# A trunk layer's kernel: source order kept in two stretches, and the two parts of x1 laid side by side for the seven products

## Chip, core and metric

The kernel runs on one core of one Trainium2 chip. The metric is device time in microseconds of one execution; the kernel before took a median of 2099.56 us in three runs (2097.77 to 2105.01). The profile shown here is of one further execution.

## What is computed

One decoder layer on 512 positions of width 2048, everything in float32. The part that the change touches is the first normalisation and projection, and the MLP at the end:

```python
def reference(x, attn_norm, w_in, sgu_w, sgu_b, conv_w, q_norm, k_norm, w_out,
              mlp_norm, w_mlp_in, w_mlp_out):
    for l in range(DEPTH):                       # DEPTH = 1
        h = rms_norm(x, attn_norm[l])
        p = h @ w_in[l]                          # 2048 -> 5632
        ...
        x = x + jnp.concatenate([y_a, y_b, y_c], axis=-1) @ w_out[l]
        h = rms_norm(x, mlp_norm[l])
        x = x + jnp.square(jax.nn.relu(h @ w_mlp_in[l])) @ w_mlp_out[l]   # 2048 -> 8192 -> 2048
    return x
```

## The kernel before

All activations lie transposed: 128 of the 2048 features on the partitions, the 512 positions along the free axis. A float32 product is made of three matmuls in the type fp32r: every operand is split into a high part (a cast by ACT, line 242) and a low part (what is left, a subtraction by DVE, line 243), and `mm3` (lines 153 to 157) adds high times high, high times low and low times high into one PSUM bank. So each weight tile needs one ACT instruction and one DVE instruction (`wh` and `wl` in the profile, from the raw tile `wr` or `wq`) before TensorE can use it. x1, the input of the MLP, is kept as `xhl`: first all high parts `xh`, then all low parts `xl`.

`stream` (line 206) runs through a list of groups. Each group is a list of pieces of weights; the loads, casts and subtractions of a piece are written two pieces ahead of its matmuls (`AHEAD`), and three buffers each hold `wr`, `wh` and `wl`. Between the matmuls, `step` takes one small piece of other work from a queue of tasks. The framework's scheduler is free to put the instructions of an engine in another order than that in which they are written; each engine then works its list strictly from the front.

The groups in order, with the stretch of the profile in which TensorE runs them:

- four groups for q and k (the first group loads x itself, splits it, line 245, and the mean squares of x come from a second copy of x, `xn`, that POOL loads, lines 264 to 269), then v, the gating and the convolution, then the output projection: 0 to about 734 us;
- the first product of the MLP, x1 times `w_mlp_in`, 8192 columns. One group of 512 columns, 29 groups of 256 columns in the Strassen-Winograd form (764 to 1345 us) and one last group of 256 columns. A group of this form needs seven products of half-size blocks instead of eight. The sums of x1's blocks are made once (tile `tt`), those of the weights by DVE for each group (lines 798 to 804). `product` (line 811) runs the matmuls: products 0, 1 and 3 have a bank of their own, and one matmul takes the high and the low part of x1 next to each other (512 columns, line 823) and a second adds the low part of the weights (256 columns, line 824). Products 2 and 4 share a bank, and so do 5 and 6; these four use `mm3` with 256 columns. DVE puts the products together in the tile `c` (line 829), of which there is one buffer, and POOL stores it in DRAM as `hd` (line 853);
- the second product, relu squared times `w_mlp_out`, from 1366 us to the end: four chunks of 2048 hidden rows (`c`), four groups of 512 outputs each (`ng`), 16 groups in all. POOL loads a hidden tile from DRAM (`hs<-hd`, or `hr` for the first eight, line 875), DVE squares and scales it (lines 879 and 880), ACT and DVE split it into `hid` or `xhl`. These are the tasks of `hid_tasks` (line 867); those of chunk c+1 are put on the queue at group 1 of chunk c. At the end of a group DVE adds its four banks to `acc` (line 925). There are six banks and a group takes four, so the third of the next group's four column blocks needs one of them back.

Of the kernel before, what the change touches and what calls it, by code (L numbers as in the profile page):

```python
# [15 lines left out]
P = 128  # L16
T = 512
# [23 lines left out]
def trunk_kernel(  # L41
# [46 lines left out]

    def step():
        if tasks:  # L90
            f = tasks.popleft()
            if f is not None:
                f()
# [28 lines left out]
    xh, xl = xhl[:, 0], xhl[:, 1]  # L122
    rstd = cpool.tile([P, TB], F32, name="rstd")
# [5 lines left out]
    def load_w(src, n, first=False):  # L129
# [5 lines left out]
        if first:  # L135
            for k in range(2):
                nc.sync.dma_start(out=first[0][:, k], in_=first[1][:, k])
                nc.sync.dma_start(out=raw[:, k], in_=src[:, k])
            for k in range(2):
                nc.vector.tensor_copy(out=h[:, k], in_=raw[:, k])  # L140
                split_x(k, first[0][:, k], g_attn)
                nc.vector.tensor_tensor(out=l[:, k], in0=raw[:, k], in1=h[:, k].bitcast(F32), op=ALU.subtract)
            return h, l
# [9 lines left out]
    def mm3(ps, a, b, start, stop):  # L153
# [3 lines left out]
        nc.tensor.matmul(ps, lhsT=al, rhs=bh, start=False, stop=stop)  # L157
# [18 lines left out]
    def tr_group(src, nt, mov, close, order=None, before=None, tail=False):  # L176
# [13 lines left out]
        def mm(k, h, l, which=None):  # L190
            for n, (j, ts) in enumerate(parts):
                if which in (None, n):
                    s = slice(j * P, (j + 1) * P)
                    a, b = mov(order[k])
                    mm3(st[n][:, ts], (h[:, s], l[:, s]), (a[:, ts], b[:, ts]), k == 0, k == KT - 1)
# [45 lines left out]
    def split(dst_h, dst_l, src):  # L241
        nc.scalar.copy(out=dst_h, in_=src)  # L242
        nc.vector.tensor_tensor(out=dst_l, in0=src, in1=dst_h.bitcast(F32), op=ALU.subtract)  # L243

    def split_x(k, src, gain):

        nc.scalar.activation(out=xh[:, k], in_=src, func=AF.Copy, scale=gain[:, k:k + 1])
        nc.vector.scalar_tensor_tensor(
            out=xl[:, k], in0=src, scalar=gain[:, k:k + 1], in1=xh[:, k].bitcast(F32), op0=ALU.mult, op1=ALU.subtract,
        )  # L250
# [13 lines left out]
    def x_tokens(i):  # L264
# [3 lines left out]
        nc.gpsimd.dma_start(out=xn_t, in_=xn_v[:, t, half * DH:(half + 1) * DH])  # L268
        return lambda: nc.scalar.activation(out=xn_t, in_=xn_t, func=AF.Square, accum_out=tok[:, t, half:half + 1])
# [104 lines left out]
    def x_chunk(kp):  # L374
# [6 lines left out]
        for n in range(2):  # L381
            split_x(2 * kp + n, xr[:, n], g_attn)

    def x_statistics():
        squares = [x_tokens(i) for i in range(3)]

        def one(i):
            squares[i]()
            if i + 3 < 2 * TB:
                squares.append(x_tokens(i + 3))  # L390

        for i in range(2 * TB):
# [11 lines left out]
    def evac_qk(pss, which, half):  # L404
        gain = q_gain if which == 0 else k_gain
# [322 lines left out]
    def close_out(pss, ng):  # L728

        xg = mlp["xg"]  # L730
        for j in range(4):
# [7 lines left out]
            split_x(n, xg[:, n], g_mlp)  # L739
            tasks.append(lambda n=n: nc.scalar.activation(out=xg[:, n], in_=xg[:, n], func=AF.Copy, scale=g_mlp[:, n:n + 1]))  # L740
        if ng == 3:
            yc["cm"].__exit__(None, None, None)
            mlp["tcm"] = pool("sums")
            tt = mlp["tt"] = mlp["tcm"].__enter__().tile([P, 2, 4, KT // 2, TH], F32R, name="tt")
# [9 lines left out]
    def x_sums(tt, xv, m, j):  # L754
# [5 lines left out]
        split(tt[:, 0, j, s], tt[:, 1, j, s], out)  # L760

    def x_operand(j, m):

        if j < 3:
            k, t = ((0, 0), (1, 0), (1, 1))[j]
            return xhl[:, :, 2 * m + k, t * TH:(t + 1) * TH]
        return mlp["tt"][:, :, j - 3, m]

    class Strassen:
# [41 lines left out]
        def product(self, j, h, l):  # L811
            sp, i = mlp["spool"], self.i
            bank, half = ((0, None), (1, None), (2, 0), (3, None), (2, 1), (4, 0), (4, 1))[j]
            if bank == len(self.banks):
                self.banks.append(main_ps(f"pt{bank}{i}"))
            ps = self.banks[bank]
            pv = ps.rearrange("p (h t) -> p h t", h=2)
# [12 lines left out]

            if j == 0:
# [3 lines left out]
                nc.scalar.copy(out=self.p[0], in_=pv[:, 0])  # L835
                add(self.p[0], pv[:, 1], self.p[0])
                return
            c = self.c
            if j == 1:
                add(c[:, 2], pv[:, 0], self.p[0])  # L840
                add(c[:, 2], pv[:, 1], c[:, 2])
            elif j == 2:
                add(c[:, 0], pv[:, 0], self.p[0])
            elif j == 3:
                nc.scalar.copy(out=self.p[1], in_=pv[:, 0])
                add(self.p[1], pv[:, 1], self.p[1])
# [8 lines left out]
    def close_mlp_in(pss, f0):  # L855

        for j, ps in enumerate(pss):
# [3 lines left out]
            nc.scalar.copy(out=c, in_=ps.rearrange("p (h t) -> p h t", h=2))  # L861
# [5 lines left out]
    def hid_tasks(c, ks, alloc, ahead):  # L867
# [9 lines left out]
        def rest(n):  # L877
            t, k = room.pop(n), ks[n]
            nc.vector.scalar_tensor_tensor(out=t, in0=t, scalar=0.0, in1=t, op0=ALU.max, op1=ALU.mult)
            nc.vector.tensor_tensor(out=t, in0=t, in1=rbc, op=ALU.mult)  # L880
# [7 lines left out]
    def open_last_in():  # L888
        mlp["tcm"].__exit__(None, None, None)
# [124 lines left out]
```

## Time and profile before

| | |
|---|---|
| median of three runs | 2099.56 us |
| profiled execution, own time | 2101.5 us |
| its span | 2099.8 us |
| TensorE (PE) busy | 2067.3 us, 98% |
| VectorE (DVE) busy | 1145.1 us, 55% |
| ScalarE (ACT) busy | 674.7 us, 32% |
| mean granted TensorE clock | 0.992 of full speed |

Busy time of PE counts a matmul from its start to its modelled end, and matmuls overlap; the pace of a stream of matmuls is read from the distance between their starts. PE stands for the matmuls, PEld for the loading of their stationary operands. A number in brackets behind a row of the timeline is the idle time of that engine ahead of it, with the instruction that ended it.

### The profile page before, as it was taken

What the parts mean: (1) busy time and instruction counts of PE and PEld (TensorE: products, weight loads), DVE (VectorE), ACT (ScalarE), POOL (GpSimd) and SP (SyncE); (2) the same over time, 40 slices, a digit from 0 to 9 for tenths busy, and PEclk for the clock granted to TensorE, in tenths of its full rate; (3) what the DMA queues carried; (4) which work ended last, traced back from release to release, by engine and by line L of the source; (5) the groups of instructions that cost most, each with busy time, mean ns of one, the idle gap of its engine ahead of it and who ended that gap; (6) DMA issues with size and microseconds to landing.
All of it is one profiled execution on the core that took longest, in us unless ns stands there. A gap on an engine that the chain in (4) does not pass through costs nothing.

```text
span 2099.8 us, 27447 instructions
## 1 busy us (share of the span) xinstructions
PE 2067.3 (98%) x11202; PEld 1807.8 (86%) x11202; DVE 1145.1 (55%) x1530; ACT 674.7 (32%) x905; POOL 100.6 (5%) x194
## 2 busy tenths in 40 slices
PE   9999999999999999999999999999989998999999
PEld 8999888888888889999999999977878887888888
DVE  5443453534335578878888788767372254322222
ACT  6233442322234434334333343432221222221221
POOL 1000000100000000000000000131010010000000
PEclk9999999999999999999999999999999999999999
DMA  8223222433533454444444444474343343233332
GB/s 276 90 76 111 71 71 68 128 96 96 188 119 126 125 161 131 131 140 122 140 131 124 138 131 126 127 254 151 112 150 96 95 133 112 92 101 97 114 120 81
DMA packets 247023, 259.81 MB, mean 124 GB/s; under 512 B 11748, under 2 KB 179940, under 8 KB 246896
## 3 DMA queue, kind: packets, MB, share of 16 engines
q1 hardware_dynamic: 229888, 206.08, 32.6%
q0 software_dynamic: 14560, 47.75, 6.5%
q10 hardware_dynamic: 2448, 4.23, 0.6%
q8 instruction: 88, 1.44, 0.3%
q14 instruction: 39, 0.32, 0.0%
HBM read 232.81 MB, written 25.19 MB: 123 GB/s over the span
## 4 chain that ended last, share of the span: by engine, by line
PE 79%; issue 16%; DMA 3%; POOL 1%; DVE 1%; SPq 0%; ACT 0%; POOLq 0%; DVEq 0%; ACTq 0%
PE pt L155 17%; PE pt L156 17%; PE pt L157 17%; PE pt L823 8%; PE pn L155 5%; PE pn L157 5%; PE pn L156 5%; PE pt L824 4%; DMA hs<-hd 1%; POOL hs L875 1%; DMA hd<-cn 1%; PE sc L505 0%; DMA wr<-in_w_in_dram 0%; PE et L518 0%; DVE wl L243 0%
## 5 line engine op out<-in xcount | busy, mean ns | idle before, releaser
L243 DVE TENSOR_TENSOR wl<-wr,wh 128x1024 fp32r<-128x1024 f32 (+2 forms) x287 | 321.4, 1120 | 652.8 <-ACT wh L242 596.5
L242 ACT CAST wh<-wr 128x1024 fp32r<-128x1024 f32 (+2 forms) x287 | 277.8, 968 | 799.6 <-PE pt L156 661.9
L155 PE MATMUL pt<-xhl,wh 128*128 128x512 f32 (+1 forms) x1144 | 419.6, 367 | 6.0 <-DVE acc L925 6.0
L156 PE MATMUL pt<-xhl,wh 128*128 128x512 f32 (+1 forms) x1144 | 418.3, 366 | 0.0
L157 PE MATMUL pt<-xhl,wl 128*128 128x512 f32 (+1 forms) x1144 | 418.1, 365 | 0.0
L155 PEld LDWEIGHTS pt<-xhl,wh 128*128 128x128 f32 x1144 | 216.5, 189 | 41.3 <-DVE acc L925 6.4
L157 PEld LDWEIGHTS pt<-xhl,wl 128*128 128x128 f32 x1144 | 216.4, 189 | 34.7
L156 PEld LDWEIGHTS pt<-xhl,wh 128*128 128x128 f32 x1144 | 216.6, 189 | 34.4 <-issue 0.2
L242 ACT CAST wh<-wq 128x1024 fp32r<-128x1024 f32 x145 | 152.0, 1048 | 250.7 <-PE pt L156 146.1
L243 DVE TENSOR_TENSOR wl<-wq,wh 128x1024 fp32r<-128x1024 f32 x145 | 177.0, 1221 | 91.2 <-ACT wh L242 91.1
L155 PE MATMUL pt<-hid,wh 128*128 128x512 f32 x512 | 201.7, 394 | 14.7 <-DVE acc L925 14.7
L157 PE MATMUL pt<-hid,wl 128*128 128x512 f32 x512 | 201.3, 393 | 2.1 <-DVE wl L243 2.0
L156 PE MATMUL pt<-hid,wh 128*128 128x512 f32 x512 | 201.2, 393 | 0.0
L155 PE MATMUL pt<-tt,wh 128*128 128x256 f32 x696 | 197.0, 283 | 0.3 <-DVE c L829 0.3
L157 PE MATMUL pt<-tt,wl 128*128 128x256 f32 x696 | 197.1, 283 | 0.0
L156 PE MATMUL pt<-tt,wh 128*128 128x256 f32 x696 | 197.0, 283 | 0.0
L155 PE MATMUL pn<-wh,xhl 128*128 128x384 f32 (+2 forms) x512 | 187.3, 368 | 4.4 <-DVE wh L140 3.8
L156 PE MATMUL pn<-wl,xhl 128*128 128x384 f32 (+2 forms) x512 | 180.4, 352 | 0.0
L157 PE MATMUL pn<-wh,xhl 128*128 128x384 f32 (+2 forms) x512 | 180.2, 352 | 0.0
L823 PE MATMUL pt<-xhl,wh 128*128 128x512 f32 x464 | 165.2, 398 | 0.0
L155 PEld LDWEIGHTS pt<-tt,wh 128*128 128x128 f32 x696 | 132.7, 191 | 3.1 <-issue 0.6
L157 PEld LDWEIGHTS pt<-tt,wl 128*128 128x128 f32 x696 | 132.9, 191 | 0.0
(210 smaller groups left out, 2933.5 us busy)
## 6 DMA issues: line engine op xcount, KB each, us to landing
wr<-in_w_mlp_out_dram SPq DMA_DIRECT2D x128, 512.0 KB, 3.6
wq<-in_w_mlp_in_dram SPq DMA_DIRECT2D x116, 512.0 KB, 4.1
wr<-in_w_in_dram SPq DMA_DIRECT2D x144, 128.0 KB, 2.4
wr<-in_w_out_dram SPq DMA_DIRECT2D x32, 512.0 KB, 3.6
hd<-c POOLq DMA_DIRECT2D x58, 256.0 KB, 2.6
hs<-hd POOLq DMA_DIRECT2D x56, 256.0 KB, 3.4
wr<-in_w_in_dram SPq DMA_DIRECT2D x24, 512.0 KB, 3.5
wr<-in_w_in_dram SPq DMA_DIRECT2D x31, 384.0 KB, 3.2
```

The costliest lines, as they stand in the source:

```text
L155: nc.tensor.matmul(ps, lhsT=ah, rhs=bh, start=start, stop=False)
L156: nc.tensor.matmul(ps, lhsT=ah, rhs=bl, start=False, stop=False)
L157: nc.tensor.matmul(ps, lhsT=al, rhs=bh, start=False, stop=stop)
L242: nc.scalar.copy(out=dst_h, in_=src)
L243: nc.vector.tensor_tensor(out=dst_l, in0=src, in1=dst_h.bitcast(F32), op=ALU.subtract)
L823: nc.tensor.matmul(pv, lhsT=h[:, m], rhs=b, start=start, stop=False)
L824: nc.tensor.matmul(pv[:, 1], lhsT=l[:, m], rhs=b[:, 0], start=False, stop=stop)
L875: nc.gpsimd.dma_start(out=room[n], in_=hd[c * KC + ks[n]])
```

## The change

Three things are changed. `ordr` marks instructions so that the scheduler keeps them in the order of the source: in the first group (until its results are evacuated) and from the opening of the last group of the first product to the end. The loads of `xn` are written singly, each tied behind the last matmul written before it (`behind`), and the squares that use them come two steps later. In the MLP the memory of `xhl` is seen as `x1v`, in which for each feature block and each half of the positions the 256 high values are followed at once by the 256 low values; `tt` gets the same form. All seven products of a group now use one matmul of 512 columns and one of 256, each in a bank of its own, and DVE adds both halves of each bank (`take`). The two plain groups of the first product read x1 through `x1mov`, as two runs of 256.

```diff
@@ load_w, split, split_x
-                nc.vector.tensor_copy(out=h[:, k], in_=raw[:, k])
-                split_x(k, first[0][:, k], g_attn)
+                ordr(nc.vector.tensor_copy(out=h[:, k], in_=raw[:, k]))
+                split_x(xh[:, k], xl[:, k], first[0][:, k], g_attn[:, k:k + 1])
...
+    def ordr(ins):
+        return tc.keep_in_program_order(ins) if ordered[0] else ins
...
+    x1v = xhl.rearrange("p s k t -> p (s k t)").rearrange("p (k h s t) -> p k h s t", k=KT, h=2, s=2)
@@ x_tokens, x_statistics
-        nc.gpsimd.dma_start(out=xn_t, in_=xn_v[:, t, half * DH:(half + 1) * DH])
+        behind(nc.gpsimd.dma_start(out=xn_t, in_=xn_v[:, t, half * DH:(half + 1) * DH]))
...
+            if i < 2 * TB:
+                squares.append(x_tokens(i))
+            if i >= 2:
+                squares[i - 2]()
@@ x_operand
-            return xhl[:, :, 2 * m + k, t * TH:(t + 1) * TH]
-        return mlp["tt"][:, :, j - 3, m]
+            return x1v[:, 2 * m + k, t]
+        return mlp["tt"][:, j - 3, m]
+
+    def x1mov(k):
+        return x1v[:, k, :, 0], x1v[:, k, :, 1]
@@ Strassen.product
-            bank, half = ((0, None), (1, None), (2, 0), (3, None), (2, 1), (4, 0), (4, 1))[j]
...
+            pv = main_ps(f"pt{j}{i}").rearrange("p (h t) -> p h t", h=2)
             for m in range(KT // 2):
+
                 b = x_operand(self.FACTOR[j], m)
-                start, stop = m == 0, m == KT // 2 - 1
-                if half is None:
-
-                    nc.tensor.matmul(pv, lhsT=h[:, m], rhs=b, start=start, stop=False)
-                    nc.tensor.matmul(pv[:, 1], lhsT=l[:, m], rhs=b[:, 0], start=False, stop=stop)
-                else:
-                    mm3(pv[:, half], (h[:, m], l[:, m]), (b[:, 0], b[:, 1]), start, stop)
+                nc.tensor.matmul(pv, lhsT=h[:, m], rhs=b, start=m == 0, stop=False)
+                nc.tensor.matmul(pv[:, 1], lhsT=l[:, m], rhs=b[:, 0], start=False, stop=m == KT // 2 - 1)
...
+            def take(out, more):
+                add(out, pv[:, 0], more)
+                add(out, pv[:, 1], out)
...
             elif j == 2:
-                add(c[:, 0], pv[:, 0], self.p[0])
+                take(c[:, 0], self.p[0])
...
             elif j == 4:
-                add(c[:, 1], pv[:, 1], c[:, 0])
+                take(c[:, 1], c[:, 0])
                 add(c[:, 0:6:5], self.p[1].unsqueeze(1).broadcast_to([P, 2, TH]), c[:, 0:2])
+            elif j == 5:
+                take(c[:, 3], c[:, 0])
             elif j == 6:
-                add(c[:, 3:5], pv, c[:, 0:2])
+                take(c[:, 4], c[:, 1])
@@ groups
-    groups.append(tr_group(w1[:, :, :T], 4, xmov, lambda pss: close_mlp_in(pss, 0)))
+    groups.append(tr_group(w1[:, :, :T], 4, x1mov, lambda pss: close_mlp_in(pss, 0)))
```

The same wrapping with `ordr` stands at every instruction of `split`, `split_x`, `hid_tasks`, the squares of `xn`, the copies of `close_mlp_in` and the additions to `acc`.

What moves in the engines' lists is shown at three places. The first is DVE inside one group of seven products, from the sum of product 3 (`p`) to the last sum of product 6 (`c`); `pt` is a bank, `wl` the low part of a product's weights. Before:

```order
L829 TENSOR_TENSOR p_7728<-pt_7789,p_7728 128x256
L829 TENSOR_TENSOR c_7726<-pt_7759,c_7726 128x256
L829 TENSOR_TENSOR c_7726<-p_7728,c_7726 128x2x256
L243 TENSOR_TENSOR wl_7850<-wq_7838,wh_7849 128x1024
L243 TENSOR_TENSOR wl_7880<-wq_7844,wh_7879 128x1024
L804 TENSOR_TENSOR wq_7844<-wq_7844,ws_7847 128x1024
L829 TENSOR_TENSOR c_7726<-pt_7853,c_7726 128x512
```

Now:

```order
L849 TENSOR_TENSOR p_7528<-pt_7582,p_7528 128x256
L849 TENSOR_TENSOR c_7526<-pt_7605,c_7526 128x256 x2
L263 TENSOR_TENSOR wl_7637<-wq_7625,wh_7636 128x1024
L849 TENSOR_TENSOR c_7526<-p_7528,c_7526 128x2x256
L849 TENSOR_TENSOR c_7526<-pt_7640,c_7526 128x256 x2
L263 TENSOR_TENSOR wl_7661<-wq_7631,wh_7660 128x1024
L832 TENSOR_TENSOR wq_7631<-wq_7631,ws_7634 128x1024
L849 TENSOR_TENSOR c_7526<-pt_7664,c_7526 128x256
L263 TENSOR_TENSOR wl_7687<-ws_7634,wh_7686 128x1024
```

Each product from 4 on is summed by two additions of 256 where one of 256 or half of one of 512 stood; over a whole group six small additions more and one of 512 fewer. The second addition of product 6 now stands behind the next group's third `wl`.

The second place is DVE at the end of the first group of the second product; `hs` are hidden tiles of the next chunk, `acc` takes the group's banks. Before:

```order
L243 TENSOR_TENSOR xhl<-hs_12618,xhl 128x512
L879 SCALAR_TENSOR_TENSOR hs_12690<-hs_12690 128x512
L243 TENSOR_TENSOR wl_12502<-wr_12500,wh_12501 128x1024
L243 TENSOR_TENSOR xhl<-hs_12654,xhl 128x512
L880 TENSOR_TENSOR hs_12690<-hs_12690,rbc 128x512
L925 TENSOR_TENSOR acc<-pt_0_12246,acc 128x512
L925 TENSOR_TENSOR acc<-pt_1_12247,acc 128x512
```

Now:

```order
L263 TENSOR_TENSOR hid<-hs_11629,hid 128x512
L263 TENSOR_TENSOR wl_11687<-wr_11685,wh_11686 128x1024
L263 TENSOR_TENSOR wl_11717<-wr_11715,wh_11716 128x1024
L263 TENSOR_TENSOR wl_11747<-wr_11745,wh_11746 128x1024
L263 TENSOR_TENSOR wl_11777<-wr_11775,wh_11776 128x1024
L950 TENSOR_TENSOR acc<-pt_0_11521,acc 128x512
L950 TENSOR_TENSOR acc<-pt_1_11522,acc 128x512
```

Before, six whole tiles of the next chunk and the start of a seventh stood ahead of the additions; now only tiles of the present chunk and weights do, and the next chunk follows behind.

The third place is ACT where the first product ends; `cn` are the two results of its last group, `hid<-hr` the casts of the first eight hidden tiles, `hid<-hs` that of the ninth. Before:

```order
L242 CAST hid<-hr_12131 128x512
L242 CAST wh_12156<-wr_12155 128x2x256
L242 CAST wh_12178<-wr_12177 128x1024
L242 CAST wh_12200<-wr_12199 128x1024
L861 COPY cn_12221<-pt_0_12028 128x512
L242 CAST wh_12241<-wr_12240 128x1024
```

Now:

```order
L262 CAST wh_11475<-wr_11474 128x1024
L262 CAST hid<-hr_11406 128x512
L885 COPY cn_11496<-pt_0_11303 128x512
L885 COPY cn_11496<-pt_1_11304 128x512
L262 CAST wh_11516<-wr_11515 128x1024
L262 CAST hid<-hs_11509 128x512
```

Three weight casts stood between the last `hr` cast and the copies of `cn`; now the copies follow it directly.

## Rows read from the trace of the kernel before

**Rows 1.** Busy time by stretch: us, PE, PEld, DVE, ACT, POOL, clock, DMA, GB/s.

```profile
950.00:1000.00 50.00, 50.00 (x364) 47.32 (x363) 40.91 (x50) 19.93 (x23) 2.15 (x4) 1.00 0.42 127
```

**Rows 2.** Waits of PE: engine, line, waited for: total us, times, longest.

```profile
PE pt L155 <- DVE acc L925: 20.7, 3, 7.5
PE pn L155 <- DVE wh L140: 3.8, 1, 3.8
PE pt L157 <- DVE wl L243: 2.0, 2, 1.1
```

**Rows 3.** Timeline of PE inside one group of seven products: start, us, instruction.

```profile
1002.04 0.28 PE L155 MATMUL pt<-tt,wh 128*128 128x256 f32 x1
...
1004.92 0.40 PE L823 MATMUL pt<-xhl,wh 128*128 128x512 f32 x1
...
1010.57 0.28 PE L155 MATMUL pt<-tt,wh 128*128 128x256 f32 x1
...
1013.46 0.40 PE L823 MATMUL pt<-tt,wh 128*128 128x512 f32 x1
...
1016.27 0.28 PE L155 MATMUL pt<-tt,wh 128*128 128x256 f32 x1
```

**Rows 4.** Timeline of DVE in the same stretch.

```profile
1003.20 1.23 DVE L243 TENSOR_TENSOR wl<-wq,wh 128x1024 fp32r<-128x1024 f32 x1 [1.55 <-ACT wh L242]
...
1005.61 0.68 DVE L829 TENSOR_TENSOR c<-pt,c 128x512 f32<-128x512 f32 x1
...
1017.48 1.23 DVE L243 TENSOR_TENSOR wl<-wq,wh 128x1024 fp32r<-128x1024 f32 x1 [1.58 <-ACT wh L242]
...
1019.35 0.42 DVE L829 TENSOR_TENSOR c<-pt,c 128x256 f32<-128x256 f32 x1 [0.31 <-PE pt L157]
```

**Rows 5.** Timeline of ACT in the same stretch.

```profile
1002.12 1.05 ACT L242 CAST wh<-wq 128x1024 fp32r<-128x1024 f32 x1 [1.83 <-PE pt L156]
```

**Rows 6.** The stores of line 853, from issue to landing.

```profile
DMA to landing us min/median/max: 2.3/2.6/4.0
```

**Rows 7.** Timeline of PE in the second product, around its second stall.

```profile
1545.37 0.39 PE L157 MATMUL pt<-hid,wl 128*128 128x512 f32 x1
...
1554.89 0.39 PE L157 MATMUL pt<-xhl,wl 128*128 128x512 f32 x1
1561.26 0.79 PE L155 MATMUL pt<-xhl,wh 128*128 128x512 f32 x1 [5.98 <-DVE acc L925]
...
1567.26 0.39 PE L157 MATMUL pt<-xhl,wl 128*128 128x512 f32 x1
```

**Rows 8.** Timeline of PE: first and last matmul of the second product.

```profile
1366.48 0.39 PE L155 MATMUL pt<-hid,wh 128*128 128x512 f32 x1
...
2095.99 0.28 PE L157 MATMUL pt<-xhl,wl 128*128 128x256 f32 x1
```

**Rows 9.** Timelines of DVE, ACT and POOL where the second product begins.

```profile
1351.42 0.69 DVE L879 SCALAR_TENSOR_TENSOR hr<-hr 128x512 f32<-128x512 f32 x1 [1.62 <-DMA hr<-hd]
...
1352.88 0.62 ACT L242 CAST hid<-hr 128x512 fp32r<-128x512 f32 x1 [2.11 <-DVE hr L880]
...
1366.00 0.59 ACT L861 COPY cn<-pt 128x512 f32<-128x512 f32 x1 [1.21 <-PE pt L157]
...
1368.32 0.55 POOL L862 DMA_DIRECT2D hd<-cn  x1 [0.89 <-ACT cn L861]
1372.94 1.61 POOL L875 DMA_DIRECT2D hs<-hd  x3 [4.08 <-DMA hd<-cn]
...
1375.95 1.29 DVE L879 SCALAR_TENSOR_TENSOR hs<-hs 128x512 f32<-128x512 f32 x2 [1.75 <-DMA hs<-hd]
```

**Rows 10.** Timeline of PE in the first group.

```profile
12.02 0.66 PE L155 MATMUL pn<-wh,xhl 128*128 128x384 f32 x1 [3.78 <-DVE wh L140]
...
16.55 1.26 PE L155 MATMUL pn<-wh,xhl 128*128 128x384 f32 x4
```

More of the change, by code (lines that the diff above doesn't have):

```diff
@@ L139, in load_w @@
             for k in range(2):
-                nc.vector.tensor_copy(out=h[:, k], in_=raw[:, k])
-                split_x(k, first[0][:, k], g_attn)
-                nc.vector.tensor_tensor(out=l[:, k], in0=raw[:, k], in1=h[:, k].bitcast(F32), op=ALU.subtract)
+                ordr(nc.vector.tensor_copy(out=h[:, k], in_=raw[:, k]))
+                split_x(xh[:, k], xl[:, k], first[0][:, k], g_attn[:, k:k + 1])
+                ordr(nc.vector.tensor_tensor(out=l[:, k], in0=raw[:, k], in1=h[:, k].bitcast(F32), op=ALU.subtract))
             return h, l
@@ L156, in mm3, with behind @@
         nc.tensor.matmul(ps, lhsT=ah, rhs=bl, start=False, stop=False)
-        nc.tensor.matmul(ps, lhsT=al, rhs=bh, start=False, stop=stop)
+        last[0] = nc.tensor.matmul(ps, lhsT=al, rhs=bh, start=False, stop=stop)
+    last = [None]
+    def behind(ins):
+        tc.add_manual_dep(
+            ins.ins, last[0].ins.name, mybir.DependencyInfo(mybir.DependencyClass.Sync, mybir.DependencyReason.DATA),
+            reason="behind",
+        )
+        return ins
     def pieces_of(src, n, order):
@@ L194, in mm @@
                     a, b = mov(order[k])
+                    if len(a.shape) == 3:
+                        mm3(st[n].rearrange("p (h t) -> p h t", h=2), (h[:, s], l[:, s]), (a, b), k == 0, k == KT - 1)
+                        continue
                     mm3(st[n][:, ts], (h[:, s], l[:, s]), (a[:, ts], b[:, ts]), k == 0, k == KT - 1)
@@ L241, in split, with split_x @@
     def split(dst_h, dst_l, src):
[L242 to L250, printed above, removed]
+        ordr(nc.scalar.copy(out=dst_h, in_=src))
+        ordr(nc.vector.tensor_tensor(out=dst_l, in0=src, in1=dst_h.bitcast(F32), op=ALU.subtract))
+    def split_x(dst_h, dst_l, src, gain):
+        ordr(nc.scalar.activation(out=dst_h, in_=src, func=AF.Copy, scale=gain))
+        ordr(nc.vector.scalar_tensor_tensor(
+            out=dst_l, in0=src, scalar=gain, in1=dst_h.bitcast(F32), op0=ALU.mult, op1=ALU.subtract,
+        ))
     def rsqrt(dst, v, s, y):
@@ L381, in x_chunk @@
         for n in range(2):
-            split_x(2 * kp + n, xr[:, n], g_attn)
+            k = 2 * kp + n
+            split_x(xh[:, k], xl[:, k], xr[:, n], g_attn[:, k:k + 1])
     def x_statistics():
-        squares = [x_tokens(i) for i in range(3)]
+        squares = []
         def one(i):
[L388 to L392, printed above, removed]
+            if i < 2 * TB:
+                squares.append(x_tokens(i))
+            if i >= 2:
+                squares[i - 2]()
+        for i in range(2 * TB + 2):
             tasks.extend([lambda i=i: one(i), None])
@@ L743, in close_out @@
             mlp["tcm"] = pool("sums")
-            tt = mlp["tt"] = mlp["tcm"].__enter__().tile([P, 2, 4, KT // 2, TH], F32R, name="tt")
+            tt = mlp["tt"] = mlp["tcm"].__enter__().tile([P, 4, KT // 2, 2, TH], F32R, name="tt")
             xv = xg.rearrange("p (m k) (h t) -> p m k h t", k=2, h=2)
@@ L759, in x_sums @@
         nc.vector.tensor_tensor(out=out, in0=a, in1=b, op=ALU.subtract)
-        split(tt[:, 0, j, s], tt[:, 1, j, s], out)
+        split(tt[:, j, s, 0], tt[:, j, s, 1], out)
     def x_operand(j, m):
@@ L955, in trunk_kernel @@
     groups.append(tr_group(
-        w1[:, :, DFF - 2 * P:], 2, xmov, lambda pss: close_last_in(pss, DFF // P - 2), before=open_last_in,
+        w1[:, :, DFF - 2 * P:], 2, x1mov, lambda pss: close_last_in(pss, DFF // P - 2), before=open_last_in,
     ))
```

40 lines of the change are left out of this document (20 added, 20 removed).

## The prediction

> **What bounds the kernel now.** I read the busy table first: TensorE is busy nearly all the time, so time can only go where its matmuls become fewer or cheaper, or where it stands still. In the table by stretches the groups of seven products show PE at 50.00 of 50 us, clock 1.00, with DVE at 40.91, or 82% [rows 1]; there PE is the bound and DVE is next. The table of waits then says where PE stands still: 20.7 us in three waits for `acc`, 3.8 us in one wait for a weight cast, 2.0 us in two waits for `wl` [rows 2]. The last view is the timeline, for the pace: I take distances between starts, since a matmul's own duration overlaps its neighbours.
>
> Seven products. A product by `mm3` is 24 matmuls of 256 columns and takes 1004.92 − 1002.04 = 2.88 us, 120 ns each. Products 0 and 1 are 16 pairs of 512 and 256 columns in 1010.57 − 1004.92 = 5.65 us, 353 ns a pair; product 3 is 8 pairs in 1016.27 − 1013.46 = 2.81 us [rows 3]. A group is 4 × 2.88 + 5.65 + 2.81 = 19.98 us, and there are 29.
>
> Second product. Undisturbed, 42 matmuls of 512 take 1554.89 − 1545.37 = 9.52 us, 226.7 ns each [rows 7]. It has 4 × 4 × 16 × 4 × 3 = 3072 of them, of which the last 48 are cut in two, 96 of 256 columns: 3024 × 0.2267 + 96 × 0.120 = 697.0 us. It takes 2095.99 + 0.12 − 1366.48 = 729.6 us [rows 8]. So 32.6 us are lost: 20.7 + 2.0 in waits [rows 2], and most of the rest behind the three long ones. [...]
>
> **The change, part by part.** My sum is made against the profiled execution's own 2101.5 us, 1.7 above its span and 1.9 above the median, which I subtract at the end.
>
> *Products merged.* Columns stay the same: three of 256 against 512 plus 256. What goes is one matmul in three. At the present pace of a pair the group would take 7 × 8 × 0.3525 = 19.74 us, 0.24 less, 7.0 us over 29 groups. That is the lower end. But the pair is dearer than its halves: 226.7 + 120 = 346.7 ns [rows 3, 7]. In the present pairs the 512 columns are read as two runs of 256 lying 32 KB apart; after the change they are one run. I take the two runs as the cause of the missing 6 ns, since nothing else about the 512-column matmul differs from those of the second product. Then the group takes 56 × 0.3467 = 19.42 us, 0.56 less: 16.2 us. The same 6 ns is then lost where x1 is read in two runs: 64 × 3 + 32 × 3 = 288 matmuls of the two plain groups, +1.8 us. Net −14.4 (ends: −7 and −17).
>
> [...]
>
> *DVE under it.* DVE has 3.44 us idle in a group: 1.55 + 1.58 + 0.31 [rows 4], so 16.54 of work. It gets six additions of 256 more (0.42 each) and one of 512 less (0.68): 16.54 + 2.52 − 0.68 = 18.4 us. Against 19.42 that fits, with 1.0 us to spare. The order must fit too. A split can start about 1.16 us after PE leaves a product (ACT starts at 1002.12 for the product that ends at 1002.04, DVE at 1003.20) [rows 4, 5] and is due two products, 5.5 us, after that; following the new list by hand from one group's third `wl` to the next, DVE comes round in PE's period, and no `wl` is later than 1.7 us before it is due. I cost it at nothing; the cover is that 1.0 us. `c` has one buffer: its last addition now ends about 2.7 us after product 6, its store lands 0.5 + 2.6 us later (up to 4.0) [rows 6], and the next group's first sum comes about 6.6 us after product 6. That just holds. Each product having its own bank costs nothing: six banks rotate, and one is free again within a product.
>
> *Second product in source order.* The additions to `acc` now stand ahead of the next chunk's tiles, and the third column block of a group finds its bank 1.4 us after the group's end, when the first addition (0.69 us) is done. So the three long waits go with their slow restarts. In steady chunks a piece asks DVE for one split, 1.2, and one hidden tile, 2.7 (from line 879 at 1351.42 through ACT's cast, ended at 1353.50, to the low part, 0.6) [rows 9], 3.9 in the 5.44 us of 24 matmuls. Nothing waits there.
>
> The start does. In the last group of the first product DVE must do 2.7 + 0.6 us for each piece, and PE needs only 12 × 0.227 = 2.7. So the eighth tile's cast, which was done before PE ended, now ends some 5.5 us after PE's end (S), and ACT's copies of `cn` stand behind it. The second store of `cn` was issued at S + 1.8 and the `hs` loads waited for it until 4.6 us later, their first use 3.0 after that [rows 8, 9]; now about S + 7, S + 11.2 and S + 14.2. Behind that first use, in source order, stand two tiles (5.4 us) and then the `wl` of the fourth piece, 1.2: S + 20.8. PE needs it after three pieces, at S + 16.3. Then 2 × 2.7 + 1.2 = 6.6 us of DVE for each of three more pieces against 5.44. That leaves PE about 4.5 + 3 × 1.15 = 8 us late. This is a new wait of `pt` on the split. Of 32.6 us lost, 8 remain: −24.6 (ends: −20 and −30, the latter if nearly nothing waits).
>
> *First group.* Three loads of `xn` (1.5 MB) no longer run beside the first x and weights. PE stood idle for 3.8 us until the cast at 12.02, and then took until 16.55 for 12 matmuls, which at full clock take 12 × 0.173 = 2.1 [rows 10] (384 columns lie midway between 256 and 512, so 173 ns is the mean of 120 and 226.7). If the second weights land before PE has done its first twelve, 8.2 us, 3.8 + 2.4 = 6.2 us are to be had; the next pieces then come sooner than their x, so I keep 1.2 back: −5 (ends: 0 and −6). The later squares wait for PE's progress, but PE needs their result only for transposes that stay where they were in its list: nothing.
>
> **Sum.** −14.4 − 24.6 − 5 = −44: 2101.5 − 44 = 2057.5 for an execution like the profiled one, 2055.6 as a median. I say 2056.
>
> **The rivals.**
>
> *The two runs cost nothing.* Then the merged pair keeps its present 352.5 ns, the products bring 7.0 instead of 16.2, and the plain groups lose nothing: −7 − 24.6 − 5 = −36.6, 2063 us. For it: product 3's pair is already a little cheaper (351 ns) than product 0's (353) with runs just as far apart. Against it: the 6 ns need another cause. [...]
>
> *Source order gives the waits back.* DVE and ACT may no longer go round a late load. If the start of the second product costs 20 us instead of 8, with the clock falling in it, 12 of the gain go: 2068. Against it: loads are issued three tiles ahead, 16 us in steady chunks.
>
> *DVE takes over in the seven products, and the kernel gets slower.* If DVE's 3.44 us of waits stayed in full on top of 18.4, since they hang on casts that follow PE, the group would take 21.8 us, 1.8 more than now: +53 − 24.6 + 1.8 − 5 = +25, 2125 us. It decides from about 20.9 us a group, where 29 × 0.95 eats up the other gains. Against it: work added in front of such a wait shortens it, and the list followed by hand does so.
>
> *The order doesn't bind where it should.* Ruled out: the lists show the additions ahead of the tiles.
>
> **Chances.** Forecast 0.62, equal runs 0.20, waits given back 0.12, DVE as the bound 0.06 (two thirds of that slower, the rest near no change). The range takes in the first three with their ends: −14.4 to −17, −24.6 to −30 and −5 to −6 give 2046 below, and I go to 2043; above, −7, −14 and −4 give 2074. A measurement of this kernel can tell about 0.3%, 6.3 us, from no change: faster 0.93, same 0.03, slower 0.04.
>
> **What would show it.** In the profile after: 232 matmuls of 512 columns for each of the seven products and no `mm3` of 256 in that stretch; starts 226 to 228 ns apart before a 256 (forecast) or 232 to 235 (equal runs); groups 19.4 or 19.7 us apart; DVE busy near 47 of 50 us there with no PE wait on `wl` or `c`. In the second product no wait on `acc`, but one on `wl` or `wh` some 16 us after its first matmul, 3 to 5 us long, with shorter ones behind it, and 697 + 8 us in all. In the first group no wait near 8 us. I am wrong if groups are longer than 19.98 us, if `acc` is still waited for, or if the wait at the second product's start is above 12 us.

## The result

The changed kernel takes a median of 2066.7 us (2066.6 to 2067.1, four runs); the kernel before took 2098.66 beside it. The ratio is 0.9842, 95% interval 0.9822 to 0.9862: 32 us faster, a change under 2% but clear of the noise. The forecast was 2056 with a range of 2043 to 2074, so the time lies in the range, 10.7 us above the forecast.

The profiled execution has a span of 2064.9 us, 34.9 less than the one of before (which took 2101.5 us, 2.8 above the median beside it). Where they went is read from four starts of matmuls. In the kernel before, the first matmul of the first group of seven products and the first one behind the last such group are

```profile
764.54 0.39 PE L823 MATMUL pt<-xhl,wh 128*128 128x512 f32 x1
...
1344.70 0.40 PE L155 MATMUL pt<-xhl,wh 128*128 128x512 f32 x1
```

and the second product runs from 1366.48 to 2095.99 [rows 8]. The same four in the timeline of PE after (start, us, instruction), with the starts of two groups in between:

```profile
758.68 0.39 PE L845 MATMUL pt<-xhl,wh 128*128 128x512 f32 x1
...
998.93 0.40 PE L845 MATMUL pt<-xhl,wh 128*128 128x512 f32 x1
...
1018.72 0.40 PE L845 MATMUL pt<-xhl,wh 128*128 128x512 f32 x1
...
1332.48 0.40 PE L162 MATMUL pt<-xhl,wh 128*128 128x512 f32 x1
...
1354.26 0.39 PE L162 MATMUL pt<-hid,wh 128*128 128x512 f32 x1
...
2061.06 0.28 PE L164 MATMUL pt<-xhl,wl 128*128 128x256 f32 x1
```

(The rows at 998.93 and 1018.72 open the same product of two successive groups: 19.79 us a group.)

| stretch | before, us | after, us | difference | forecast |
|---|---|---|---|---|
| start to the first group of seven products | 764.5 | 758.7 | −5.9 | −5 + 1.2 |
| 29 groups of seven products | 580.2 | 573.8 | −6.4 | −16.2 |
| last plain group of the first product | 21.8 | 21.8 | 0.0 | +0.6 |
| second product, first to last start | 729.5 | 706.8 | −22.7 | −24.6 |

So two of the three terms came nearly as worked out, and the products brought 6.4 us instead of 16.2. The busy table by stretches after shows PE full and DVE busier than before, 45.81 for the 40.91 of [rows 1], with PE at full clock:

```profile
950.00:1000.00 50.00, 50.00 (x285) 43.32 (x285) 45.81 (x63) 19.91 (x23) 3.24 (x6) 1.00 0.46 139
```

In the waits of PE neither `acc` nor the first weight cast of [rows 2] is left; there is one new row (total us, times, longest):

```profile
PE pt L162 <- ACT wh L262: 6.9, 3, 4.6
```

PE's timeline shows these three waits where the second product starts, and the slow restart behind the first (1375.81 to 1379.36 holds 9 matmuls, 3.55 us instead of 2.04; the granted clock there is 0.58):

```profile
1370.78 0.39 PE L164 MATMUL pt<-hid,wl 128*128 128x512 f32 x1
1375.81 0.79 PE L162 MATMUL pt<-hid,wh 128*128 128x512 f32 x1 [4.64 <-ACT wh L262]
...
1379.36 0.39 PE L162 MATMUL pt<-hid,wh 128*128 128x512 f32 x1
...
1389.60 0.50 PE L162 MATMUL pt<-hid,wh 128*128 128x512 f32 x1 [1.14 <-ACT wh L262]
...
1396.50 0.50 PE L162 MATMUL pt<-hid,wh 128*128 128x512 f32 x1 [1.14 <-ACT wh L262]
```

What they wait for is read from the timelines of ACT, POOL and DVE after, in this order. PE leaves the first product at 1354.26, but ACT casts the eighth hidden tile only at 1360.51, and everything else stands behind it: the copies of `cn`, their stores, the loads of `hs`, the first use of one, and then the cast of the fourth piece's weights at 1374.72:

```profile
1360.51 0.62 ACT L262 CAST hid<-hr 128x512 fp32r<-128x512 f32 x1 [2.62 <-DVE hr L904]
1361.03 1.07 ACT L885 COPY cn<-pt 128x512 f32<-128x512 f32 x2
...
1374.72 1.04 ACT L262 CAST wh<-wr 128x1024 fp32r<-128x1024 f32 x1
```

```profile
1361.90 1.08 POOL L886 DMA_DIRECT2D hd<-cn  x2 [17.53 <-ACT cn L885]
1365.91 1.60 POOL L899 DMA_DIRECT2D hs<-hd  x3 [2.92 <-DMA hd<-cn]
```

```profile
1339.54 0.69 DVE L263 TENSOR_TENSOR hid<-hr,hid 128x512 fp32r<-128x512 f32 x1 [0.69 <-ACT hid L262]
...
1342.85 0.69 DVE L263 TENSOR_TENSOR hid<-hr,hid 128x512 fp32r<-128x512 f32 x1 [0.69 <-ACT hid L262]
...
1369.99 0.69 DVE L903 SCALAR_TENSOR_TENSOR hs<-hs 128x512 f32<-128x512 f32 x1 [5.69 <-DMA hs<-hd]
```

The two `hid` rows of DVE are 3.31 us apart, where PE needs 2.72 for a piece: that is why the eighth tile is late.

Two rows settle the point on which the term of the products rested. In the last plain group x1 is now read as two runs of 256:

```profile
1346.78 0.39 PE L162 MATMUL pt<-xhl,wh 128*128 128x512 f32 x1
...
1353.58 0.39 PE L162 MATMUL pt<-xhl,wh 128*128 128x512 f32 x1
```

Thirty matmuls lie between them: 6.80 / 30 = 226.7 ns, the pace of one run [rows 7]. Two runs cost nothing, and the merged pairs, whose 512 columns are now one run, still take 19.79 / 56 = 353.4 ns. So the 6 ns above 226.7 + 120 have another cause. The experiments look for it, then for the waits at the second product's start.

### The profile page after: what moved, and what is told of

Read it like the earlier page. It is cut to its first block, busy times and chain, and to the rows that moved or that the text cites. A ratio compares the mean times of both kernels' runs of the same rounds, so it can differ in the third digit from the quotient of the medians.

```text
span 2064.9 us, 25736 instructions
## 1 busy us (share of the span) xinstructions
PE 2051.5 (99%) x10274; PEld 1751.2 (85%) x10274; DVE 1198.2 (58%) x1675; ACT 677.5 (33%) x905; POOL 100.6 (5%) x194
## 4 chain that ended last, share of the span: by engine, by line
PE 71%; issue 26%; POOL 2%; DMA 0%; DVE 0%; ACT 0%; POOLq 0%; DVEq 0%; ACTq 0%
PE pt L162 18%; PE pt L163 18%; PE pt L164 18%; PE pn L162 5%; PE pn L163 5%; PE pn L164 5%; POOL hd L877 1%; PE pt L845 1%; PE pt L846 1%; PE sc L529 0%; PE et L542 0%; PE qt L463 0%; ACT wh L262 0%; DMA acc<-x1d 0%; PE warm L124 0%
## 5 line engine op out<-in xcount | busy, mean ns | idle before, releaser
L162 PE MATMUL pt<-xhl,wh 128*128 128x512 f32 (+1 forms) x912 | 352.6, 387 | 0.0
L163 PE MATMUL pt<-xhl,wh 128*128 128x512 f32 (+1 forms) x912 | 351.6, 386 | 0.0
L164 PE MATMUL pt<-xhl,wl 128*128 128x512 f32 (+1 forms) x912 | 351.5, 385 | 0.0
L845 PE MATMUL pt<-tt,wh 128*128 128x512 f32 x928 | 330.5, 399 | 0.0
L846 PE MATMUL pt<-tt,wl 128*128 128x256 f32 x928 | 260.6, 281 | 0.0
L845 PE MATMUL pt<-xhl,wh 128*128 128x512 f32 x696 | 248.5, 399 | 0.0
L845 PEld LDWEIGHTS pt<-tt,wh 128*128 128x128 f32 x928 | 174.4, 188 | 43.6
L162 PEld LDWEIGHTS pt<-xhl,wh 128*128 128x128 f32 x912 | 171.3, 188 | 34.6 <-issue 0.2
L164 PEld LDWEIGHTS pt<-xhl,wl 128*128 128x128 f32 x912 | 171.3, 188 | 34.6
L163 PEld LDWEIGHTS pt<-xhl,wh 128*128 128x128 f32 x912 | 171.3, 188 | 34.2 <-issue 0.2
L846 PE MATMUL pt<-xhl,wl 128*128 128x256 f32 x696 | 195.5, 281 | 0.0
L846 PEld LDWEIGHTS pt<-tt,wl 128*128 128x128 f32 x928 | 175.3, 189 | 0.0
```

The costliest lines, as they stand in the source:

```text
L162: nc.tensor.matmul(ps, lhsT=ah, rhs=bh, start=start, stop=False)
L163: nc.tensor.matmul(ps, lhsT=ah, rhs=bl, start=False, stop=False)
L164: last[0] = nc.tensor.matmul(ps, lhsT=al, rhs=bh, start=False, stop=stop)
L845: nc.tensor.matmul(pv, lhsT=h[:, m], rhs=b, start=m == 0, stop=False)
```

## The experiments

Each edit is made in the changed kernel unless it says otherwise. Ratios are to the kernel before, run on the same chip.

**The parts apart.** The products (banks and sums included) and x1's layout are put back as in the kernel before, the reverse of those parts of the diff that stands ahead; of the change remain these lines and their like:

```diff
+        return tc.keep_in_program_order(ins) if ordered[0] else ins
...
+        behind(nc.gpsimd.dma_start(out=xn_t, in_=xn_v[:, t, half * DH:(half + 1) * DH]))
```

> Only the two parts that set the order (second product and first group, with the loads of xn tied behind matmuls) are kept; products and the layout of x1 are those of the kernel before. Theory: the parts add up. The trace after shows the groups of seven products 7.0 us shorter in all (29 x 0.24), so this kernel should be 7 us above the changed one: 2073.7 us (2071.5 to 2076). Rival, the order is worth what it is only with the merged products (their banks, their DVE list): then it loses more, above 2078, with a wait on acc or a longer wait at the start of the second product. Rival, the merged products are worth more than their pace shows: above 2076 with the same waits as the changed kernel.

Measured 2073.41 us (ratio 0.9878, 0.9861 to 0.9894), waits 5.6 us on the weight cast and 0.7 on a sum. The parts add up: the order (with the later loads of `xn`) is worth some 26 us, the merged products 6.7.

**The old layout.** These lines, and with them the splits that write x1 and `tt`; the plain groups read one run again.

```diff
-            return x1v[:, 2 * m + k, t]
-        return mlp["tt"][:, j - 3, m]
+            return xhl[:, :, 2 * m + k, t * TH:(t + 1) * TH]
+        return mlp["tt"][:, :, j - 3, m]
```

> The changed kernel with x1 and its sums in the old layout (all high parts, then all low parts), so that the 512 columns of a merged matmul are again two runs of 256 that lie 32 KB apart; all seven products stay merged, and the two plain groups read one run of 512. Theory now: runs cost nothing, a pair stays 352 to 353 ns, 2066.7 us (2065.5 to 2068). Rival, the prediction's cause: two runs cost 6 ns a pair against one run; since the trace after shows 353 ns for one run, two runs would then take 359, 1624 pairs x 6 ns = +9.7 us, 2076.

Three runs took 2066.8 to 2067.4 us, so the layout makes no difference. A fourth took 2055.9, which neither theory has; another such run, further below, has a trace.

**512 first, then 256.**

```diff
                 nc.tensor.matmul(pv, lhsT=h[:, m], rhs=b, start=m == 0, stop=False)
+            for m in range(KT // 2):
+                b = x_operand(self.FACTOR[j], m)
                 nc.tensor.matmul(pv[:, 1], lhsT=l[:, m], rhs=b[:, 0], start=False, stop=m == KT // 2 - 1)
```

> The changed kernel, but inside each product the eight matmuls of 512 columns stand first and the eight of 256 after them. Theory: the 6 ns of a pair hang on the alternation of 512 and 256. Then a product takes 8 x 226.7 + 8 x 120 ns and one change of width, 2.78 us for 2.825, 203 products: -9 us, 2057.5 us (2056 to 2060), groups 19.45 us apart, if DVE, with 18.3 us of work in a group, still keeps up. If DVE does not keep up: groups 19.55 to 19.75 and waits of PE on wl or wh, 2060 to 2065. Rival: the 256-column matmul of this form (it adds to half a bank) or the 512 behind it is dearer by itself, whatever stands beside it: 2066.7 us, no change.

Measured 2059.70 us (0.9812, 0.9797 to 0.9827): 7.0 of the 9 expected, with no wait of PE in the groups. PE's timeline of one product:

```profile
1001.73 2.00 PE L845 MATMUL pt<-tt,wh 128*128 128x512 f32 x8
1003.57 1.12 PE L848 MATMUL pt<-tt,wl 128*128 128x256 f32 x8
1004.53 0.86 PE L845 MATMUL pt<-tt,wh 128*128 128x512 f32 x3
```

The eight matmuls of 256 take 0.96 us, 120 ns each; the eight of 512 take 1.84, 230 each instead of 226.7. Sorting the widths gives most of the 6 ns a pair back; the one change to 512 that each product keeps still costs 0.03 us.

**The other half of the bank.**

```diff
-                nc.tensor.matmul(pv[:, 1], lhsT=l[:, m], rhs=b[:, 0], start=False, stop=m == KT // 2 - 1)
+                nc.tensor.matmul(pv[:, 0], lhsT=l[:, m], rhs=b[:, 0], start=False, stop=m == KT // 2 - 1)
```

> The changed kernel, but the matmul of 256 columns adds to the first half of the bank instead of the second (DVE adds both halves, so the sum is the same). Theory (alternation of widths): no change, 2066.7 us (2065.5 to 2068), pairs 353 ns. Rival: the 6 ns come from adding to the half of the bank that the 512-column matmul before has only just finished writing; the first half is 107 ns older, so the pair falls to 346.7 ns, 1624 x 6 ns = -9.7, 2057 us.

Measured 2066.81 us: no change. What the matmul before has just written is not the cause. (The rival's 107 ns are an estimate, the difference of the two measured paces: 226.7 − 120.)

**The low part one tile later.** In `hid_tasks` the subtraction of a tile stands between the two steps of the next tile; the cast stays behind the scaling of its own tile.

```diff
-            split(d[:, 0, k], d[:, 1, k], t)
+            if n:
+                u, q = room.pop(n - 1), ks[n - 1]
+                ordr(nc.vector.tensor_tensor(out=d[:, 1, q], in0=u, in1=d[:, 0, q].bitcast(F32), op=ALU.subtract))
...
+                ordr(nc.scalar.copy(out=d[:, 0, k], in_=t))
```

> The changed kernel, but the low part of a hidden tile is subtracted one tile later, between the two steps of the next tile, so that DVE no longer stands 0.69 us waiting for ACT's cast of the same tile. Theory: the remaining waits at the start of the second product (6.9 us in three, and 1.5 us of slow matmuls behind the first) come from DVE's pace, 3.31 us a piece against PE's 2.72 before the start and 6.9 against 5.44 behind it; with about 2.65 and 5.5 the copies of the last two results come some 4.5 us sooner and the waits fall below 2 us in all: 2059.5 us (2058 to 2062). Rival: the chain copies, store, load of the ninth tile sets the start, whatever DVE's pace: the first wait stays above 3 us and only the two of 1.1 go, 2064.5 us. Rival 2: the delayed subtraction holds up tiles in the steady chunks (loads come one tile later): new waits there, 2067 or more.

Three runs took 2069.5 to 2070.0 us, 2.8 more than the changed kernel, so this theory fell; the waits on the weight cast grew from 6.9 to 9.1 us. DVE's timeline shows why:

```profile
1330.07 0.69 DVE L263 TENSOR_TENSOR wl<-wr,wh 128x512 fp32r<-128x512 f32 x1 [1.21 <-ACT wh L262]
...
1333.77 0.69 DVE L263 TENSOR_TENSOR wl<-wr,wh 128x512 fp32r<-128x512 f32 x1 [1.21 <-ACT wh L262]
```

A piece now takes 3.70 us. ACT still casts the tile ahead of the weights, and the subtraction that used to fill DVE's time until then has been moved away: the wait grew from 0.69 to 1.21 and moved to `wl`.

The fourth run, the profiled one, took 2058.87 although it has those waits. Its pairs run at 353.4 ns until this place, with a 256-column matmul that lasts 0.36 us instead of 0.28, with no wait shown (PE's timeline):

```profile
767.29 0.39 PE L845 MATMUL pt<-tt,wh 128*128 128x512 f32 x1
767.52 0.36 PE L846 MATMUL pt<-tt,wl 128*128 128x256 f32 x1
767.71 0.39 PE L845 MATMUL pt<-tt,wh 128*128 128x512 f32 x1
```

Two products later, and until the last group ends, every product runs at 346.6 to 346.8 ns a pair: the forecast's number, with the same instructions. 1624 pairs by 6.8 ns are 11.0 us, about the distance of this run from its three companions (10.6 to 11.2), and that of the odd run with the old layout (10.9 to 11.4), of which there is no trace.

**Both.** The order of widths and the later low part, and the ninth hidden tile one piece later in the list:

```diff
-        tasks.extend(hid_tasks(0, range(KC // 2, KC), hid_room, 3))
+        tasks.extend([None, None] + hid_tasks(0, range(KC // 2, KC), hid_room, 3))
```

> The delayed subtraction, the eight matmuls of 512 columns ahead of the eight of 256 in every product, and the ninth hidden tile one piece later in the list, behind the split of the fourth piece's weights. Theory: the gains add, 7.0 for the order of widths (measured) and 8 for the start of the second product: 2051.5 us (2050 to 2054), with no wait of PE above 1 us behind the first product. Rival: a start without waits is not reached because the first use of the ninth tile still stands ahead of weights: 2055.

Measured 2058.84 us (0.9808, 0.9793 to 0.9822), 0.9 below the order of widths alone and above both expected ranges. The longest wait fell to 1.9 us, four waits of 5.1 in all stayed: the piece of 3.7 us is still there.

**The early loads back.** `behind` is taken from the loads of `xn`.

```diff
-        behind(nc.gpsimd.dma_start(out=xn_t, in_=xn_v[:, t, half * DH:(half + 1) * DH]))
+        nc.gpsimd.dma_start(out=xn_t, in_=xn_v[:, t, half * DH:(half + 1) * DH])
```

> The changed kernel, but the loads of xn are no longer tied behind matmuls; the order of the source is kept as in the changed kernel. Theory (the prediction's): the first three loads of xn, 1.5 MB, again run beside the first x and weights, the wait near 8 us comes back (3 to 4 us), and what the first group gained is lost: 2072 us (2070 to 2073.5). Rival: the order of DVE and ACT gave the gain, the loads only ran alongside: no wait near 8 us, 2066.7 us (2065.5 to 2068).

Measured 2077.0 us (2074.3 to 2078.6; 0.9893, 0.9877 to 0.991), more than either theory has. PE's timeline in the first group:

```profile
9.34 0.41 PE L162 MATMUL pn<-wh,xhl 128*128 128x384 f32 x1 [1.18 <-DVE wh L147]
...
13.93 0.88 PE L162 MATMUL pn<-wh,xhl 128*128 128x384 f32 x4
...
48.07 0.69 PE L162 MATMUL pn<-wh,xhl 128*128 128x384 f32 x1 [3.72 <-DVE qn L440]
```

The wait near 8 us is back with 1.18 us, not 3.8. The second piece starts at 13.93; it was 16.55 before [rows 10] and is 9.91 in the changed kernel. Of the 6.6 us the loads are worth 4.0 with the order kept; by difference the order is worth 2.6. Most of the rest of the 10 us lost here lies in a second wait, at 48.07, for the evacuation `qn`: in DVE's list it now stands behind the statistics of x, which are not ahead of it in the changed kernel. So taking `behind` away changed the list too, and the 10 us are not the loads' alone.

**More work for DVE.**

```diff
                 nc.vector.tensor_tensor(out=self.s1, in0=q[1, 0], in1=q[1, 1], op=ALU.add)
+                nc.vector.tensor_tensor(out=self.s1, in0=q[1, 0], in1=q[1, 1], op=ALU.add)
+                nc.vector.tensor_tensor(out=self.s1, in0=q[1, 0], in1=q[1, 1], op=ALU.add)
```

> The changed kernel, but DVE forms the first sum of the weights (128x1024, 1.22 us) three times instead of once in each group of seven products: 2.44 us more of its work, the same result. DVE works 18.1 us of a group of 19.79 and idles 1.66. Theory (idle time in front of a wait is taken up by added work): the group becomes 18.1 + 2.44 = 20.6 us with no idle time of DVE left, 0.8 more than now: 29 x 0.8 = +23, 2090 us (2084 to 2097). Rival (the prediction's case in which DVE takes over: its waits for casts stay in full): 18.1 + 2.44 + 1.45 = 22.0 us a group, +64, 2131 us.

Measured 2087.6 us, one run, in the range of the first theory. PE now waits 22 times for a `wl` in the 29 groups, and in its timeline two of these waits are 20.76 us apart:

```profile
PE pt L848 <- DVE wl L263: 10.7, 22, 0.6
```

```profile
980.26 0.38 PE L848 MATMUL pt<-xhl,wl 128*128 128x256 f32 x1 [0.58 <-DVE wl L263]
...
1001.02 0.39 PE L848 MATMUL pt<-xhl,wl 128*128 128x256 f32 x1 [0.57 <-DVE wl L263]
```

DVE's waits for casts were swallowed by the added work. One idle row of DVE is left in such a group, 1.35 us for the store of `c`, whose single buffer is due there:

```profile
1010.78 0.42 DVE L851 TENSOR_TENSOR c<-pt,p 128x256 f32<-128x256 f32 x1 [1.35 <-DMA hd<-c]
```

So the 20.76 us are 19.4 of work and this wait, which first shows at 865.79 us, ahead of PE's first at 918.27. The theory's "no idle time of DVE left" did not hold, and its 20.6 came near by luck: 19.4 us of work alone would have fitted into PE's 19.79.

**An extra matmul in each group.**

```diff
+            if j == 3:
+                nc.tensor.matmul(
+                    pv[:, 0, :(self.c0 - T) // (2 * P) * 8 + 8], lhsT=h[:, 0], rhs=x_operand(self.FACTOR[j], 0)[:, 0, :(self.c0 - T) // (2 * P) * 8 + 8], start=True, stop=True)
```

> The changed kernel, with one extra matmul ahead of product 3 in each of the 29 groups, into the bank that the product then overwrites; its width grows from 8 columns in the first group to 232 in the last, so that the stream of pairs is shifted once a group by another amount. In one execution of the kernel with the later low part the pairs, which are the same instructions as in the changed kernel, ran at 346.6 ns after a hiccup of 0.08 us, and at 353.4 in the others. Theory: the stream of pairs has two steady patterns, 353.4 and 346.6 ns, and a disturbance decides which one follows: the pace changes between these two values from group to group, and never lies between them for long; about 2066.8 + 3 (the extra matmuls) - 0.38 us for each group that runs in the shorter pattern, 2059 to 2070 us. Rival: the pattern is a property of the execution (its memory, its clock), not of the stream: all groups at 353.4 (2070 us) or all at 346.6 (2059 us).

Measured 2064.9 us, one run, as the first theory has it. The pace of the products behind the extra matmul, from the distances of their first matmuls:

| columns of the extra matmul | pairs until the next one, ns |
|---|---|
| 8, 16, 24, 32, 40, 48, 56 | 346.6 to 346.8 |
| 64, 72 | 352.4 to 353.9 |
| 80, 104, 120, 152, 168, 184, 200, 216, 232 | 346.6 to 346.8 |
| 88, 96, 112, 128, 136, 144, 160, 176, 192, 208, 224 | 352.4 to 353.9 |

Nothing lies between the two values; each is reached within the product that follows the extra matmul and kept until the next one. So in this run the same stream of pairs had two steady paces, and what came ahead of it decided between them. That was not the width alone. Of the first seven only the one of 8 columns met the longer pace, and the others left the shorter one in place. From 64 columns on, all nine that met the shorter pace led to the longer one, and nine of the thirteen that met the longer led to the shorter.

**One extra matmul in the whole program.**

```diff
+            if j == 3 and self.c0 == T:
+                nc.tensor.matmul(pv[:, 0, :16], lhsT=h[:, 0], rhs=x_operand(self.FACTOR[j], 0)[:, 0, :16], start=True, stop=True)
```

> The changed kernel with one extra matmul of 16 columns in the whole program, ahead of product 3 of the first group of seven products. Theory: the stream of pairs falls into its shorter pattern there and stays in it to the end, since nothing disturbs it: 200 products of 8 pairs, 6.8 ns each, -10.9, +0.1 for the extra matmul: 2066.8 - 10.8 = 2056.0 us (2055 to 2057.5) in every run, groups 19.41 us apart. Rival: the longer pattern is where the stream returns to by itself, at a group's end or at a late weight: 2060 to 2067. Rival 2: which pattern follows is chance from run to run: runs at 2056 and runs at 2067 side by side.

Measured 2056.11 us, all four runs between 2056.07 and 2057.00 (0.9787, 0.9772 to 0.9801). PE's timeline shows the extra matmul; 230 us later a group takes 1019.10 − 999.68 = 19.42 us, the forecast's number:

```profile
767.30 0.17 PE L843 MATMUL pt<-tt,wh 128*128 128x16 f32 x1
767.33 0.48 PE L847 MATMUL pt<-tt,wh 128*128 128x512 f32 x1
...
999.68 0.39 PE L847 MATMUL pt<-tt,wh 128*128 128x512 f32 x1
...
1019.10 0.39 PE L847 MATMUL pt<-tt,wh 128*128 128x512 f32 x1
```

The distances of single pairs show what the two paces are made of. In the changed kernel they are 349, 350 and 361 ns in turn, through all the groups; here each is 346 or 347. In the odd execution with the later low part, 343 and 350 take turns, with the same mean. Four pairs in PE's timeline of the changed kernel:

```profile
1000.35 0.40 PE L845 MATMUL pt<-xhl,wh 128*128 128x512 f32 x1
...
1000.70 0.40 PE L845 MATMUL pt<-xhl,wh 128*128 128x512 f32 x1
...
1001.05 0.40 PE L845 MATMUL pt<-xhl,wh 128*128 128x512 f32 x1
...
1001.41 0.40 PE L845 MATMUL pt<-xhl,wh 128*128 128x512 f32 x1
...
1001.76 0.40 PE L845 MATMUL pt<-tt,wh 128*128 128x512 f32 x1
```

**The cast one step later too.** The order of widths, and two edits in the hidden tiles (`tasks.extend([None, None] + ...)` puts the ninth one piece later; `rest` becomes this):

```diff
+            if n:
+                u, q = room.pop(n - 1), ks[n - 1]
+                ordr(nc.scalar.copy(out=d[:, 0, q], in_=u))
+            if n < len(ks):
+                t = room[n]
+                ordr(nc.vector.scalar_tensor_tensor(out=t, in0=t, scalar=0.0, in1=t, op0=ALU.max, op1=ALU.mult))
+            if n:
+                ordr(nc.vector.tensor_tensor(out=d[:, 1, q], in0=u, in1=d[:, 0, q].bitcast(F32), op=ALU.subtract))
+                load(n - 1 + ahead)
+            if n < len(ks):
+                ordr(nc.vector.tensor_tensor(out=t, in0=t, in1=rbc, op=ALU.mult))
```

> Eight matmuls of 512 columns ahead of the eight of 256 in each product (2059.7 us by itself), the ninth hidden tile one piece later in the list, and, other than in the kernel with the later low part, the cast of a hidden tile too comes one step later, behind the cast of the next weights, so that neither DVE nor ACT waits for the other inside a piece. Theory: in the last group of the first product a piece then takes DVE 0.72 + 3 x 0.6 = 2.6 us against PE's 2.72 (it was 3.31, and 3.71 with only the low part later), the copies of the last results come 1 to 2 us after PE's end, the first hidden tile of the second part some 12 us after it, and no wait of PE above 0.5 us is left there: 2059.7 - 8.4 = 2051.3 us (2050 to 2053.5). Rival: the chain from the copies over the store to the loads and the adds stays too long, one wait of 1 to 3 us is left with a slow restart: 2053.5 to 2057.

Measured 2050.34 us (0.976, 0.9744 to 0.9776), 9.4 below the order of widths alone; PE is left with no wait on the weight cast. From the kernel of **Both**, which took 2058.84 us, only the place of the cast differs.

**The extra matmul and the later cast.**

> The extra matmul, and the later start of the hidden tiles' second half (its cast and low part one step later, the ninth tile one piece later), without the new order of widths. Theory: the gains add: 2066.8 - 10.8 - 9.4 = 2046.6 us (2045.5 to 2048), 3.7 below the kernel with the order of widths. Rival: DVE, with 18.1 us of work in 19.41, holds up a split in some group, the stream falls back into the longer pattern: 2050 to 2057.

Measured 2046.39 us (2046.29 to 2046.75; 0.974, 0.9724 to 0.9756): the fastest here, 20 us below the changed kernel. By the timelines of DVE and PE a piece of the last plain group takes DVE 2.72 us, PE's own pace, and the second product runs for 2040.85 + 0.12 − 1343.78 = 697.2 us; the prediction's undisturbed sum was 697.0.

```profile
1333.57 0.69 DVE L263 TENSOR_TENSOR wl<-wr,wh 128x512 fp32r<-128x512 f32 x1 [0.22 <-ACT wh L262]
...
1336.29 0.69 DVE L263 TENSOR_TENSOR wl<-wr,wh 128x512 fp32r<-128x512 f32 x1 [0.22 <-ACT wh L262]
```

```profile
1343.78 0.39 PE L162 MATMUL pt<-hid,wh 128*128 128x512 f32 x1
...
2040.85 0.28 PE L164 MATMUL pt<-xhl,wl 128*128 128x256 f32 x1
```

## Why the prediction was right or wrong

**The products: mis-sized, by a wrong cause.** The step that failed is "I take the two runs as the cause of the missing 6 ns, since nothing else about the 512-column matmul differs". Something else did: it stands beside a 256, and in these runs such a stream settled either at 353.4 ns a pair or at 346.6. The two runs are refuted twice, by the plain group at 226.7 ns and by the old layout at the same time. So the pair kept 353.4 ns, where 346.7 was forecast, and the term brought 6.4 us instead of 16.2. The rival of equal runs was the right one, and its 7.0 us is close to the 6.4 in the trace and the 6.7 between medians; the +1.8 for the plain groups did not come. The time fell into the range because the range took that rival in.

The number itself, 346.7, was not wrong as a price of the work: it is the shorter of two paces of the same stream. By their times the changed kernel's four runs all had the longer one, and with one matmul of 16 columns ahead it takes 2056.1 us. That the forecast of 2056 reappears there is partly luck: the first stretch was off by −2.1 us, the last plain group by −0.6 and the second product by +1.9, which nearly cancel. The longer pace was seen only where the widths alternate, but their alternating does not force it; what in PE makes a stream keep one pace or the other is not shown by these runs.

**DVE under the products: right.** 18.4 us of work in a group was forecast. Busy time is 45.81 / 50 × 19.79 = 18.1, and DVE did not hold PE up even at 19.42 us. The tripled sum is no second measure of this work, since 1.35 of its 20.76 us are idle: what gave way first was the single buffer of `c`, of which the prediction said "That just holds". The rival in which its waits stay in full fell with the tripled sum: 20.76 us a group, where it wanted 22.0.

**The second product: right in place and size.** The waits on `acc` went and the predicted new one came, one after another as listed from S, PE's end of the first product (1354.26): loads of `hs` at S + 11.7 (forecast 11.2), first use S + 15.7 (14.2), PE back at S + 21.6 (20.8), late by 4.64 (4.5), then 1.14 twice (1.15 three times). It was due on the cast and not on the subtraction behind it, which is the same chain. 706.8 + 0.1 − 697.0 = 9.9 us remain lost where 8 were expected; the slow restart of 1.5 us behind the first wait (granted clock 0.58) was left out of the sum. In the kernel before, the restart behind the second long wait [rows 7] ran at a granted clock of 0.52: 14 matmuls in 6.00 us, where 14 × 0.2267 = 3.17 would do. The rival of waits given back (20 us) was too dark.

**First group: right, a little low.** 5.9 us for 5, and 6.6 at the second piece, of which 0.8 go later. The reason was incomplete: the loads are 4.0 of the 6.6, the order, by difference, the rest.

## What to carry to other kernels

Where two engines hand work back and forth in one fixed order, move the whole step, not half of it: delaying the subtraction alone made the start slower (3.31 to 3.70 us a piece); delaying the cast with it, and the ninth tile by a piece, removed every wait of PE there. And before a few nanoseconds are put down to the one difference that one sees, look for the same operation elsewhere in the trace with that difference alone. The trace before had none (its two runs always stood beside a 256), so the 6 ns were an open point; the plain group of the trace after settled it. One extra matmul was worth 10.6 us, the layout nothing.

## What was not expected of the hardware

- In these runs the stream of alternating 512- and 256-column matmuls kept one of two steady paces, 353.4 ns a pair (the changed kernel, 758.68 to 1332.48 us) or 346.6 (with one extra matmul, from 767.33 to the end of the groups), with the same instructions and the same granted clock of 1.00. At the longer one the pairs repeated in threes (349, 350, 361 ns). A hiccup of 0.08 us or an extra matmul moved it from one to the other: one of 16 columns led to the shorter pace in eight runs of eight (by their times), and those of 64 columns and more that met the shorter pace led back to the longer, nine of nine.
- Behind a change from 256 to 512 columns the eight matmuls of 512 in a product took 1.84 us; at 226.7 ns each they would take 1.81.
- Work of DVE that no longer fitted a group showed late: with 2.44 us added, PE waited 22 times for a `wl` in the 29 groups, the first time at 918.27 us.
